# A fixed order for all engines in the second half of a down-projection

## The chip, the cores and the metric

The kernel runs on one core of a Trainium2 chip. The metric is the device time of one execution in microseconds, lower is better. All data are float32; one launch computes the whole layer.

## The reference, cut to what matters

The layer is a hybrid of two recurrent mixers with a convolutional feed-forward block behind them. The change lies in the last piece: the down-projection of the feed-forward block, its residual sum and the final norm.

```python
def _conv_ffn(h, w_up, conv_w, w_down, rows, cols):
    u = _dwconv2d(h @ w_up, conv_w, rows, cols)
    a, b = jnp.split(u, 2, axis=-1)
    return (jax.nn.silu(a) * b) @ w_down          # (1024, 2816) @ (2816, 1024)

xl = xl + g2 * _conv_ffn(...)                     # residual sum, (1024 tokens, 1024)
return _rmsnorm(xl, final_norm_w)                 # y * rsqrt(mean(y*y) + EPS) * w
```

## The kernel before

The engines are called V (VectorE), S (ScalarE), G (GpSimd), PE (TensorE) and SY (SyncE, which issues the DMAs). `P` is 128, `D` is 1024, `NLT` is 8 (blocks of 128 tokens), `NF` is 22 (slices of 128 rows of the inner width 2816), `NL` is 4.

Float32 products are made in three matmuls of a short float format (`F32R`): an operand is split into a high part, which is a cast (`S.copy`), and a low part, which is the operand less its high part. `gh` and `gl` are the parts of the activations `Gt[c]` (128 x 1024), `wh` and `wl` those of the weights (128 x 512). The three products are (gh, wh), (gh, wl), (gl, wh).

`down_ops(c, dh, kind)` (L1500 to L1524) makes the four parts for slice c and output half dh: a DMA brings the weights of two slices into `wst` (three buffers), S casts `wh` (L1520) and `gh` (L1522), G subtracts for `wl` (L1521), V for `gl` (L1523). With kind 1, `gh` and `gl` go into two pairs of buffers (tags L0 to L3) that alternate with c, so that the parts of slice c can be written when the matmuls of slice c-2 have ended. With kind 2 the parts go into buffers of their own, in the places of activations that are no longer read, so that four slices are kept at once.

The output has 1024 columns and is made in two halves (`dh` 0 and 1) of 512. In each half all eight token blocks are summed up in PSUM at once, which fills it. In the loop over slices (L1578 to L1584) each slice gives 24 matmuls (three for each of eight blocks). In the first half this loop runs over all 22 slices. In the second half it runs over 18, and for the last four (`rest`, L1585) the order is turned: block by block, the 12 matmuls of four slices, so that each block can be finished while the next is computed.

Behind the first half come, for each block: `evac` (V multiplies the PSUM result by the gate `g2bc` into `ytmp`, L1595), `acc` (V adds it to the residual `ys`, L1600; S squares the sum and adds it up into `s0`, L1602), and a multiplication of the sum by the norm weight `fnw` on G (L1611). Behind each block of the second half comes `evac` and `acc` again and then `final`: G adds the two sums of squares, scales and adds EPS, and takes the power -1/2 (L1615 to L1617), S and V scale the two halves (L1618, L1619), SY issues the output DMA (L1620). `final` of block t-1 is written behind `acc` of block t.

A list scheduler decides the order of the instructions of each engine, save within `tc.manual_schedule(engines=...)`: there the engines named keep the order of the program text. Before, this held for PE in the whole down-projection, and for PE and V from L1623, the blocks of the last four slices, on. S, G and SY were ordered by the scheduler.

Of the kernel before, what the change touches and what calls it, by code (L numbers as in the profile page):

```python
# [9 lines left out]
F32 = mybir.dt.float32  # L10
F32R = mybir.dt.float32r
I32 = mybir.dt.int32
AF = mybir.ActivationFunctionType
ALU = mybir.AluOpType
# [3 lines left out]
P = 128  # L18
D = 1024
# [5 lines left out]
NLT = T // P  # L25
# [6 lines left out]
EPS = 1e-6  # L32
# [43 lines left out]
def kernel(ctx: ExitStack, tc: tile.TileContext, A: dict, out: bass.AP):  # L76
    nc = tc.nc
    ms_cm = tc.manual_schedule(engines={mybir.EngineType.PE})
    ms_cm.__enter__()
    V, S, G, PE, SY = nc.vector, nc.scalar, nc.gpsimd, nc.tensor, nc.sync  # L80

    def pool(name, bufs=1, space=None, side=None):
        kw = {}
        if space is not None:
            kw["space"] = space
        if side is not None:
            kw["side"] = side
        return tc.tile_pool(name=name, bufs=bufs, **kw)
# [3 lines left out]
    def take(units, n):  # L92
        for _ in range(n):
            next(units, None)
# [21 lines left out]
    neghalf = cst[:, P + 89:P + 96]  # L116
# [82 lines left out]
    for k in range(KD):  # L199
        for g, gs in enumerate(x7g):  # L200
            if k == 0:
                S.activation(ssq[g], xk[k][:, gs], AF.Square)
            elif k == KD - 1 or g == 0:
                w_ = gs if k == KD - 1 else slice(0, T)
                n_ = w_.stop - w_.start
                sq = sp2.tile([P, T], F32, name="sq", tag="ld", bufs=8)
# [193 lines left out]
    order = [*range(KD // 2, KD), *range(KD // 2)]  # L400
    for k in range(KD):
        n = k + 2
# [232 lines left out]
    with ExitStack() as es:  # L635
# [12 lines left out]
        acc = [0.0, 0.0]  # L648
# [191 lines left out]
        def ml_prep(h, qt):  # L840
            Wt = []
            Qs = []
            for d in range(2):
                g4 = ml4.tile([P, NLT, P], F32, name="g4", tag="w4")
                SY.dma_start(out=g4, in_=gdv[h, d * 16 + NCX:d * 16 + NCH, :].partition_broadcast(P))
                w4 = ml4.tile([P, NLT, P], F32, name="w4t", tag="w4")
                V.tensor_tensor(w4, g4, mmask[:, d, :].unsqueeze(1).to_broadcast([P, NLT, P]), op=ALU.max)
                for c in range(NLT):
                    S.activation(w4[:, c, :], w4[:, c, :], AF.Exp, scale=-1.0, bias=U[:, d, NCX + c, h:h + 1])
                G.tensor_tensor(g4, g4, M[:, d, NCX:NCH, h:h + 1].to_broadcast([P, NLT, P]), op=ALU.subtract)  # L850
                S.activation(g4, g4, AF.Exp, scale=-1.0)
                V.tensor_tensor(g4, g4, qt.rearrange("p (c t) -> p c t", c=NLT), op=ALU.mult)
                Wt.append(w4)
                Qs.append(g4)
            return Wt, Qs
# [110 lines left out]
        pre = ml_prep(0, cur["q"])  # L966
        run(rnd1)
        flips = None
        for h in range(H):
# [12 lines left out]
            pre = None  # L982
# [360 lines left out]
    with ExitStack() as es:  # L1343
# [56 lines left out]
        ms_cm = tc.manual_schedule(engines={mybir.EngineType.PE, mybir.EngineType.Activation})  # L1400
# [52 lines left out]
    def big_tile(i, name):  # L1453
        return pl_tile(name) if i % 4 < 2 else psb.tile([P, T], F32, name=name, tag="plb")
# [7 lines left out]
    with ExitStack() as es:  # L1462
# [36 lines left out]
        def down_ops(c, dh, kind):  # L1499
            if c % 2 == 0:  # L1500
                st = wp.tile([P, 2, 512], F32, name="wst", bufs=3)
                SY.dma_start(out=st, in_=A["wdown"][dh, c // 2].rearrange("p (a b) -> p a b", a=2))
                pst["s"] = st
                if kind == 2:
                    pst["w"] = [g_pool(c - NF + NL + i).tile([P, 2, 512], F32R, name="wd", tag=f"G{c - NF + NL + i}")
                                for i in range(2)]
            src = pst["s"][:, c % 2, :]
            if kind == 2:
                wh, wl = [w[:, c % 2, :] for w in pst["w"]]
                gh, gl = [g_pool(j).tile([P, T], F32R, name="gd", tag=f"G{j}")  # L1510
                          for j in range(NL + 2 * (c - NF + NL), NL + 2 * (c - NF + NL) + 2)]
            else:
                wh = wp.tile([P, 512], F32R, name="wh", bufs=4)
                wl = wp.tile([P, 512], F32R, name="wl", bufs=4)
                if kind:
                    gh, gl = [lo.tile([P, T], F32R, name="gd", tag=f"L{2 * (c % 2) + i}") for i in range(2)]
                else:
                    gh = Gr.tile([P, T], F32R, name="gh")
                    gl = Gr.tile([P, T], F32R, name="gl")
            S.copy(wh, src)  # L1520
            G.tensor_tensor(wl, src, raw(wh), op=ALU.subtract)  # L1521
            S.copy(gh, Gt[c])  # L1522
            (G if dh == 0 and c < 3 else V).tensor_tensor(gl, Gt[c], raw(gh), op=ALU.subtract)  # L1523
            return gh, gl, wh, wl  # L1524
# [30 lines left out]
    dn_ = ctx.enter_context(pool("dn", bufs=2, side="right"))  # L1555
    d1 = ctx.enter_context(pool("d1", bufs=1, side="right"))
    fnw = d1.tile([P, D], F32, name="fnw")
    SY.dma_start(out=fnw, in_=A["fnw"].partition_broadcast(P))
    ms_cm = tc.manual_schedule(engines={mybir.EngineType.PE})
    ms_cm.__enter__()  # L1560
    ys = [lo.tile([P, D], F32, name=f"y{t}", tag=f"L{4 + t}") for t in range(NLT)]
    s0 = d1.tile([P, NLT, 2], F32, name="s0")
    pre = [pre0]
    for dh in range(2):
        ds_ = slice(dh * 512, (dh + 1) * 512)
        pp = [big_tile(i, "pd") for i in range(NLT // 2)]
        po = [pp[t % 4][:, (t // 4) * 512:(t // 4 + 1) * 512] for t in range(NLT)]

        def part(c, last, dh=dh):
            return down_ops(c, dh, 2 if last else 1)  # L1570

        def mm(t, c, gh, gl, wh, wl):
            ts_ = slice(t * P, (t + 1) * P)
            for pi, (x, w) in enumerate(((gh, wh), (gh, wl), (gl, wh))):
                PE.matmul(po[t], x[:, ts_], w,  # L1575
                          start=(c == 0 and pi == 0), stop=(c == NF - 1 and pi == 2))

        n = NF - NL * dh  # L1578
        for c in range(n):
            if dh == 0 and 6 <= c < 6 + NLT:  # L1580
                SY.dma_start(out=ys[c - 6], in_=x1d[c - 6])
            ops = pre.pop(0) if pre else part(c, False)
            for t in (0, 4, 1, 5, 2, 6, 3, 7):
                mm(t, c, *ops)  # L1584
        rest = [part(c, True) for c in range(n, NF)]  # L1585

        yt = []
        slots = itertools.cycle(range(12, 16))

        def evac(t):  # L1590
            if not yt:
                pair = lo.tile([P, T], F32, name="ytmp", tag=f"L{next(slots)}")
                yt.extend((pair[:, 0:512], pair[:, 512:1024]))
            tmp = yt.pop(0)
            V.tensor_tensor(tmp, po[t], g2bc[:, ds_], op=ALU.mult)  # L1595
            return tmp

        def acc(t, tmp):
            y = ys[t][:, ds_]
            V.tensor_tensor(y, y, tmp, op=ALU.add)  # L1600
            sq = dn_.tile([P, 512], F32, name="fsq")
            S.activation(sq, y, AF.Square, accum_out=s0[:, t, dh:dh + 1])  # L1602
            return y

        if dh == 0:
            order = (0, 4, 1, 5, 2, 6, 3, 7)
            tmps = [evac(t) for t in order]
            pre = [part(c, False, 1) for c in range(2)]
            for t, tmp in zip(order, tmps):
                y = acc(t, tmp)  # L1610
                G.tensor_tensor(y, y, fnw[:, ds_], op=ALU.mult)  # L1611
            continue
        def final(t, y):
            rs = dn_.tile([P, 2], F32, name="rs")
            G.tensor_tensor(rs[:, 0:1], s0[:, t, 0:1], s0[:, t, 1:2], op=ALU.add)  # L1615
            G.tensor_scalar(rs[:, 0:1], rs[:, 0:1], 1.0 / D, EPS, op0=ALU.mult, op1=ALU.add)
            G.tensor_tensor(rs[:, 1:2], rs[:, 0:1], neghalf[:, 0:1], op=ALU.pow)  # L1617
            S.activation(ys[t][:, 0:512], ys[t][:, 0:512], AF.Copy, scale=rs[:, 1:2])  # L1618
            V.scalar_tensor_tensor(y, y, rs[:, 1:2], fnw[:, ds_], op0=ALU.mult, op1=ALU.mult)  # L1619
            SY.dma_start(out=out[t * P:(t + 1) * P, :], in_=ys[t])  # L1620

        ms_cm.__exit__(None, None, None)
        ms_cm = tc.manual_schedule(engines={mybir.EngineType.PE, mybir.EngineType.DVE})  # L1623
        ms_cm.__enter__()
        pend = None
        for t in range(NLT):
            for i, ops in enumerate(rest):
                mm(t, n + i, *ops)
            cur = (t, acc(t, evac(t)))
            if pend is not None:  # L1630
                final(*pend)
            pend = cur
        final(*pend)
    ms_cm.__exit__(None, None, None)


# [81 lines left out]
```

## Time and profile before

| | us |
|---|---|
| median of 3 runs | 1572.02 |
| lowest and highest run | 1570.85, 1574.15 |
| profiled execution, its time | 1571.65 |
| its span, first to last instruction | 1569.8 |
| TensorE busy in the span | 1498.0 |
| first down-projection matmul | 1305.7 |

The time of an execution is taken on the device and is a little longer than the span, which goes from the first to the last instruction in the profile. PE stands for matmuls, PEld for their weight loads, DVE for VectorE, ACT for ScalarE, POOL for GpSimd, SP for SyncE. All positions are microseconds from the start of the span. PEclk is the clock granted to TensorE as a share of 2.4 GHz; 0.50 is 1.2 GHz.

### The profile page before, as it was taken

What the parts mean: (1) busy time and instruction counts of PE and PEld (TensorE: products, weight loads), DVE (VectorE), ACT (ScalarE), POOL (GpSimd) and SP (SyncE); (2) the same over time, 40 slices, a digit from 0 to 9 for tenths busy, and PEclk for the clock granted to TensorE, in tenths of its full rate; (3) what the DMA queues carried; (4) which work ended last, traced back from release to release, by engine and by line L of the source; (5) the groups of instructions that cost most, each with busy time, mean ns of one, the idle gap of its engine ahead of it and who ended that gap; (6) DMA issues with size and microseconds to landing.
All of it is one profiled execution on the core that took longest, in us unless ns stands there. A gap on an engine that the chain in (4) does not pass through costs nothing.

```text
span 1569.8 us, 22515 instructions
## 1 busy us (share of the span) xinstructions
PE 1498.0 (95%) x8934; PEld 1216.9 (78%) x8934; DVE 1112.2 (71%) x1460; ACT 543.4 (35%) x949; POOL 599.6 (38%) x510
## 2 busy tenths in 40 slices
PE   7899999998999999999999999999999998998997
PEld 4667788887877777777867888888888886886886
DVE  5777667779486776766587988989889898226334
ACT  4443243444143243434454222222222223233332
POOL 0073244554244644433322433332333325335341
PEclk8999999999999999999999999999999999999999
DMA  9246430222031111125567111111111104111102
GB/s 377 84 145 199 145 98 28 80 68 55 33 119 55 56 42 44 39 82 173 176 213 287 41 54 41 54 50 45 54 41 54 52 30 160 58 50 41 51 30 108
DMA packets 47935, 141.78 MB, mean 90 GB/s; under 512 B 4947, under 2 KB 15059, under 8 KB 47830
## 3 DMA queue, kind: packets, MB, share of 16 engines
q1 hardware_dynamic: 47830, 140.35, 26.5%
q8 instruction: 70, 1.15, 0.3%
q14 instruction: 35, 0.29, 0.1%
HBM read 119.81 MB, written 12.13 MB: 84 GB/s over the span
## 4 chain that ended last, share of the span: by engine, by line
PE 70%; DVE 7%; POOL 3%; ACT 3%; issue 2%; DMA 1%; POOLq 0%; SPq 0%; ACTq 0%; DVEq 0%
PE pu L1429 30%; PE pd L1575 13%; PE po L1285 3%; PE pl_hg L509 3%; PE pl_zb L509 3%; PE pl_zf L509 3%; PE pl_mo L509 2%; PE pl_mq L509 2%; PE pc L509 1%; PE pl_hq L509 1%; PE ap L1088 1%; DVE G L1490 1%; POOL QQ L1125 1%; PE st L876 1%; PE pl_mk L509 1%
## 5 line engine op out<-in xcount | busy, mean ns | idle before, releaser
L1429 PE MATMUL pu<-low,wh 128*128 128x512 f32 x1216 | 374.2, 389 | 0.0
L133 ACT CAST wh<-wst 128x512 fp32r<-128x512 f32 x184 | 112.0, 620 | 527.9 <-issue 227.2
L135 POOL TENSOR_TENSOR wl<-wst,wh 128x512 fp32r<-128x512 f32 x114 | 150.8, 1325 | 356.0 <-ACT wh L133 343.0
L1429 PEld LDWEIGHTS pu<-low,wh 128*128 128x128 f32 x1216 | 228.2, 188 | 47.4
L1429 PE MATMUL pu<-low,wl 128*128 128x512 f32 x608 | 236.5, 389 | 0.0
L1490 DVE SCALAR_TENSOR_TENSOR G<-pu,fcw,G 128x945 f32<-128x945 f32 (+2 forms) x168 | 205.3, 1222 | 23.9 <-ACT G L1483 19.1
L1490 DVE SCALAR_TENSOR_TENSOR cb<-pu,fcw,cb 128x945 f32<-128x945 f32 (+2 forms) x168 | 205.3, 1222 | 23.6 <-ACT cb L1483 18.8
L1575 PE MATMUL pd<-wh,gd 128*128 128x512 f32 x624 | 195.8, 395 | 11.6 <-DVE gd L1523 6.7
L1523 DVE TENSOR_TENSOR gd<-G,gd 128x1024 fp32r<-128x1024 f32 x41 | 56.8, 1386 | 129.7 <-ACT gd L1522 129.5
L1575 PEld LDWEIGHTS pd<-wh,gd 128*128 128x128 f32 x624 | 118.8, 191 | 37.9 <-DVE gd L1523 7.8
L1125 POOL TENSOR_TENSOR QQ<-QQ,FF 128x256 f32<-128x256 f32 x112 | 108.8, 993 | 80.7 <-PE ap L1088 38.0
L1429 PEld LDWEIGHTS pu<-low,wl 128*128 128x128 f32 x608 | 114.1, 188 | 23.7
L1575 PE MATMUL pd<-wl,gd 128*128 128x512 f32 x312 | 122.8, 394 | 0.0
L1521 POOL TENSOR_TENSOR wl<-wst,wh 128x512 fp32r<-128x512 f32 x40 | 73.2, 1833 | 113.8 <-ACT wh L1520 113.8
L135 DVE TENSOR_TENSOR wl<-wst,wh 128x512 fp32r<-128x512 f32 x70 | 57.7, 844 | 58.1 <-ACT wh L133 57.9
L1522 ACT CAST gd<-G 128x1024 fp32r<-128x1024 f32 x43 | 45.0, 1049 | 131.4 <-PE pd L1575 124.8
L1575 PEld LDWEIGHTS pd<-wl,gd 128*128 128x128 f32 x312 | 59.6, 191 | 12.5
L1118 DVE TENSOR_TENSOR KK<-KK,FF 128x768 f32<-128x768 f32 (+1 forms) x56 | 52.2, 942 | 15.2 <-PE tps L1104 11.8
L1552 POOL TENSOR_TENSOR G<-G,cb 128x1024 f32<-128x1024 f32 x22 | 53.9, 2452 | 14.9 <-DVE cb L1490 14.9
L874 POOL TENSOR_SCALAR kw<-ktok,WS 128x128 f32<-128x128 f32 x60 | 25.2, 422 | 49.2 <-PE st L876 48.9
L330 POOL TENSOR_TENSOR wl<-wst,wh 128x512 fp32r<-128x512 f32 x18 | 31.6, 1775 | 30.8 <-ACT wh L328 22.0
L1081 ACT COPY X<-KK 128x512 f32<-128x512 f32 x40 | 26.9, 682 | 47.0 <-DVE KK L1118 34.0
(390 smaller groups left out, 3078.3 us busy)
## 6 DMA issues: line engine op xcount, KB each, us to landing
wst<-in_wup_dram SPq DMA_DIRECT2D x44, 512.0 KB, 3.3
wst<-in_wcm_dram SPq DMA_DIRECT2D x28, 512.0 KB, 3.4
wst<-in_wmod_dram SPq DMA_DIRECT2D x26, 512.0 KB, 3.4
wst<-in_wout_dram SPq DMA_DIRECT2D x24, 512.0 KB, 3.6
wst<-in_wdown_dram SPq DMA_DIRECT2D x22, 512.0 KB, 3.4
wst<-in_wvml_dram SPq DMA_DIRECT2D x10, 512.0 KB, 6.0
x<-in_xcT_dram SPq DMA_DIRECT2D x8, 512.0 KB, 6.3
wsh<-in_wsh_dram SPq DMA_DIRECT2D x8, 512.0 KB, 10.1
```

The lines of the kernel that those rows point to most:

```text
L133: S.copy(wh, st[:, hs_])
L135: (eng or G).tensor_tensor(wl, st[:, hs_], raw(wh), op=ALU.subtract)
L509: PE.matmul(o, w[:, ws], x[k][:, c0:c1], start=(k == 0 and pi == 0), stop=(k == KD - 1 and pi == 2))
L1118: V.tensor_tensor(kv, kv, tk, op=ALU.mult)
L1125: G.tensor_tensor(qv, qv, tq, op=ALU.mult)
L1285: PE.matmul(po[g], x[k][:, ts_], halves[g][wi], start=(k == 0 and pi == 0), stop=(k == KD - 1 and pi == 2))
L1429: PE.matmul(pl[:, gs], w[:, ws], x[k][:, gs], start=(k == 0 and pi == 0), stop=(k == KD - 1 and pi == 2))
L1490: V.scalar_tensor_tensor(a3[:, r0:r1, c0:c1], s3[:, r0 + dy:r1 + dy, c0 + dx:c1 + dx], wcol((dy + 1) * 3 + dx + 1), a3[:, r0:r1, c0:c1], o ...
L1521: G.tensor_tensor(wl, src, raw(wh), op=ALU.subtract)
L1523: (G if dh == 0 and c < 3 else V).tensor_tensor(gl, Gt[c], raw(gh), op=ALU.subtract)
L1552: G.tensor_tensor(Gt[j], Gt[j], cb, op=ALU.mult)
L1575: PE.matmul(po[t], x[:, ts_], w, start=(c == 0 and pi == 0), stop=(c == NF - 1 and pi == 2))
```

## The change

From the end of the first half on, PE, V, S and G all keep the order of the text. The parts of slice 0 of the second half are written before the eight evacuations of the first, the parts of slice 1 behind them, and in the loop the parts of slice c+2 behind the matmuls of slice c. The eight `acc` of the first half, which stood behind the evacuations, become a generator (`sums`), of which two are taken in each of the slices 0 to 3. The eight multiplications by `fnw` become another (`scaled`), one for each slice from 4 on, each with a small G instruction that adds EPS to the first half's sum of squares. The division by D goes into the square (`scale=D ** -0.5`). `final` loses one G instruction, and the last block's output goes out in two DMAs of 512 columns, one issued by S and one by SY. The parts of slices 18 to 21 (`rest`) stand behind the loop, as before, but are now held to that order.

```diff
-    s0 = d1.tile([P, NLT, 2], F32, name="s0")
+    s0 = d1.tile([P, NLT, 4], F32, name="s0")
...
             for t in (0, 4, 1, 5, 2, 6, 3, 7):
                 mm(t, c, *ops)
+            if dh and c + 2 < n:
+                pre.append(part(c + 2, False))
+                take(late[0], 2)
+                if c > 3:
+                    take(late[1], 1)
         rest = [part(c, True) for c in range(n, NF)]
...
-            S.activation(sq, y, AF.Square, accum_out=s0[:, t, dh:dh + 1])
+            S.activation(sq, y, AF.Square, scale=D ** -0.5, accum_out=s0[:, t, dh:dh + 1])
             return y
 
         if dh == 0:
             order = (0, 4, 1, 5, 2, 6, 3, 7)
+            ms_cm.__exit__(None, None, None)
+            ms_cm = tc.manual_schedule(engines={mybir.EngineType.PE, mybir.EngineType.DVE, mybir.EngineType.Activation,
+                                                mybir.EngineType.Pool})
+            ms_cm.__enter__()
+            pre = [part(0, False, 1)]
             tmps = [evac(t) for t in order]
-            pre = [part(c, False, 1) for c in range(2)]
-            for t, tmp in zip(order, tmps):
-                y = acc(t, tmp)
-                G.tensor_tensor(y, y, fnw[:, ds_], op=ALU.mult)
+            pre.append(part(1, False, 1))
+
+            def sums(todo, acc=acc):
+                for t, tmp in todo:
+                    acc(t, tmp)
+                    yield
+
+            def scaled(fs=fnw[:, ds_]):
+                for t in order:
+                    y = ys[t][:, 0:512]
+                    G.tensor_scalar(s0[:, t, 0:1], s0[:, t, 0:1], 1.0, EPS, op0=ALU.mult, op1=ALU.add)
+                    G.tensor_tensor(y, y, fs, op=ALU.mult)
+                    yield
+
+            late = (sums(list(zip(order, tmps))), scaled())
             continue
-        def final(t, y):
-            rs = dn_.tile([P, 2], F32, name="rs")
-            G.tensor_tensor(rs[:, 0:1], s0[:, t, 0:1], s0[:, t, 1:2], op=ALU.add)
-            G.tensor_scalar(rs[:, 0:1], rs[:, 0:1], 1.0 / D, EPS, op0=ALU.mult, op1=ALU.add)
-            G.tensor_tensor(rs[:, 1:2], rs[:, 0:1], neghalf[:, 0:1], op=ALU.pow)
-            S.activation(ys[t][:, 0:512], ys[t][:, 0:512], AF.Copy, scale=rs[:, 1:2])
-            V.scalar_tensor_tensor(y, y, rs[:, 1:2], fnw[:, ds_], op0=ALU.mult, op1=ALU.mult)
-            SY.dma_start(out=out[t * P:(t + 1) * P, :], in_=ys[t])
-
-        ms_cm.__exit__(None, None, None)
-        ms_cm = tc.manual_schedule(engines={mybir.EngineType.PE, mybir.EngineType.DVE})
-        ms_cm.__enter__()
+
+        def final(t, y, one=True):
+            G.tensor_tensor(s0[:, t, 3:4], s0[:, t, 0:1], s0[:, t, 1:2], op=ALU.add)
+            rs = dn_.tile([P, 1], F32, name="rs")
+            G.tensor_tensor(rs, s0[:, t, 3:4], neghalf[:, 0:1], op=ALU.pow)
+            S.activation(ys[t][:, 0:512], ys[t][:, 0:512], AF.Copy, scale=rs)
+            if not one:
+                S.dma_start(out=out[t * P:(t + 1) * P, 0:512], in_=ys[t][:, 0:512])
+            V.scalar_tensor_tensor(y, y, rs, fnw[:, ds_], op0=ALU.mult, op1=ALU.mult)
+            if one:
+                SY.dma_start(out=out[t * P:(t + 1) * P, :], in_=ys[t])
+            else:
+                SY.dma_start(out=out[t * P:(t + 1) * P, 512:1024], in_=y)
...
             pend = cur
-        final(*pend)
+        final(*pend, False)
```

## Rows read from the trace of the kernel before

**Rows 1.** The page, parts 1 and 2: busy time by engine, and the busy share of matmuls and the granted clock in 40 slices of the span, in tenths.
```profile
PE 1498.0 (95%) x8934; PEld 1216.9 (78%) x8934; DVE 1112.2 (71%) x1460; ACT 543.4 (35%) x949; POOL 599.6 (38%) x510
...
PEclk8999999999999999999999999999999999999999
```

**Rows 2.** Busy time by engine in stages of the second half: start and end, length, busy time and (x) instructions of each engine, then granted clock, DMA share and GB/s. The stages are: chunks 0 and 1; the stop; chunk 2; chunks 3 to 17; the last four slices by blocks; the rest of the span.
```profile
1433.59:1444.49 10.90, 10.90 (x49) 8.82 (x47) 10.90 (x11) 5.01 (x13) 7.87 (x5) 1.00 0.15 51
1444.49:1449.54 5.05, 0.16 (x1) 0.00 (x0) 3.27 (x3) 3.14 (x8) 5.05 (x4) 0.89 0.00 0
1449.54:1458.14 8.60, 8.13 (x24) 6.07 (x25) 3.85 (x2) 1.94 (x3) 6.23 (x4) 0.67 0.16 49
1458.14:1539.74 81.60, 81.60 (x362) 67.59 (x361) 27.16 (x18) 27.23 (x34) 27.52 (x16) 1.00 0.11 34
1539.74:1561.90 22.16, 22.16 (x98) 17.87 (x96) 13.67 (x20) 9.41 (x20) 5.69 (x19) 1.00 0.29 119
1561.90:1569.80 7.90, 0.05 (x1) 0.00 (x0) 2.80 (x4) 2.06 (x4) 1.81 (x6) 0.66 0.49 199
```

**Rows 3.** The list of waits from 1340 to 1570: who waited for whom, total us, times, longest us.
```profile
ACT gd L1522 <- PE pd L1575: 109.7, 30, 6.7
...
PEld pd L1575 <- ACT gd L1522: 5.3, 1, 5.3
```

**Rows 4.** The timeline of ScalarE around the boundary of the halves: start, duration, line, operation, count, and in brackets the idle time before and who ended it. The casts of L1522 write `gh` of chunk 0, 1, 2, 3 and 4 of the second half, in this order.
```profile
1428.14 1.05 ACT L1522 CAST gd<-G 128x1024 fp32r<-128x1024 f32 x1 [3.87 <-PE pd L1575]
1433.59 1.05 ACT L1522 CAST gd<-G 128x1024 fp32r<-128x1024 f32 x1 [3.87 <-PE pd L1575]
1438.10 0.63 ACT L1602 ACTIVATE fsq<-y 128x512 f32<-128x512 f32 x1 [2.94 <-DVE y L1600]
...
1447.83 0.63 ACT L1602 ACTIVATE fsq<-y 128x512 f32<-128x512 f32 x1 [0.95 <-DVE y L1600]
1448.46 1.03 ACT L1522 CAST gd<-G 128x1024 fp32r<-128x1024 f32 x1
1449.40 0.61 ACT L1520 CAST wh<-wst 128x512 fp32r<-128x512 f32 x1
1449.92 1.04 ACT L1522 CAST gd<-G 128x1024 fp32r<-128x1024 f32 x1
...
1458.19 1.05 ACT L1522 CAST gd<-G 128x1024 fp32r<-128x1024 f32 x1 [6.71 <-PE pd L1575]
```

**Rows 5.** The timelines of VectorE and GpSimd around the same place, a run of like instructions merged into one row.
```profile
1429.23 1.23 DVE L1523 TENSOR_TENSOR gd<-G,gd 128x1024 fp32r<-128x1024 f32 x1 [4.17 <-ACT gd L1522]
1430.37 4.87 DVE L1595 TENSOR_TENSOR ytmp<-pd,g2bc 128x512 f32<-128x512 f32 x8
...
1436.29 11.45 DVE L1600 TENSOR_TENSOR y<-y,ytmp 128x512 f32<-128x512 f32 x8
...
1438.90 11.19 POOL L1611 TENSOR_TENSOR y<-y,fnw 128x512 f32<-128x512 f32 x7 [1.38 <-ACT fsq L1602]
...
1452.27 3.50 POOL L1521 TENSOR_TENSOR wl<-wst,wh 128x512 fp32r<-128x512 f32 x2
```

**Rows 6.** The chain of work that ended last, from 1427 to 1455, in order of time: start, us, what.
```profile
1436.29 2.99 DVE y L1600 x4
...
1440.90 6.85 DVE y L1600 x4
```

**Rows 7.** All instructions of two lines: count, duration in ns (min/median/max), first and last start.
```profile
L1523 DVE TENSOR_TENSOR gd<-G,gd x41: 1215/1226/2296, 1327.7 to 1530.0; 128x1024 fp32r<-128x1024 f32 x41
...
L1521 POOL TENSOR_TENSOR wl<-wst,wh x40: 1277/1809/2286, 1271.0 to 1519.7; 128x512 fp32r<-128x512 f32 x40
```

**Rows 8.** The timeline of the end, behind the last matmul (blocks 6 and 7).
```profile
1562.72 0.69 DVE L1600 TENSOR_TENSOR y<-y,ytmp 128x512 f32<-128x512 f32 x1
1562.98 0.72 ACT L1618 ACTIVATE y<-y,rs 128x512 f32<-128x512 f32 x1 [1.22 <-POOL rs L1617]
...
1563.60 0.61 ACT L1602 ACTIVATE fsq<-y 128x512 f32<-128x512 f32 x1
...
1564.39 0.19 POOL L1615 TENSOR_TENSOR rs<-s 128x1 f32<-128x1 f32 x1 [1.45 <-ACT fsq L1602]
1564.67 0.19 POOL L1616 TENSOR_SCALAR rs<-rs 128x1 f32<-128x1 f32 x1
1564.94 0.55 POOL L1617 TENSOR_TENSOR rs<-rs,cst 128x1 f32<-128x1 f32 x1
1565.53 0.72 ACT L1618 ACTIVATE y<-y,rs 128x512 f32<-128x512 f32 x1 [1.22 <-POOL rs L1617]
1565.53 0.75 DVE L1619 SCALAR_TENSOR_TENSOR y<-y,rs,fnw 128x512 f32<-128x512 f32 x1 [1.46 <-POOL rs L1617]
```

**Rows 9.** The output DMAs of blocks 6 and 7: their issue on SP, and the DMA share (second figure from the end) and GB/s (last) in stages behind the issue of block 7.
```profile
1564.15 0.33 SPq L1620 DMA_DIRECT2D out_dram<-y  x1
...
1566.35 0.33 SPq L1620 DMA_DIRECT2D out_dram<-y  x1
...
1566.35:1567.05 0.70, 0.00 (x0) 0.00 (x0) 0.00 (x0) 0.00 (x0) 0.00 (x0) 0.50 0.00 0
1567.05:1568.45 1.40, 0.00 (x0) 0.00 (x0) 0.00 (x0) 0.00 (x0) 0.00 (x0) 0.50 0.91 375
1568.45:1569.80 1.35, 0.00 (x0) 0.00 (x0) 0.00 (x0) 0.00 (x0) 0.00 (x0) 0.50 0.00 0
```

**Rows 10.** The timeline of ScalarE, at the first of the casts for the last four slices (`wd`).
```profile
1502.88 0.62 ACT L1520 CAST wd<-wst 128x512 fp32r<-128x512 f32 x1 [5.05 <-DMA wst<-in_wdown_dram]
```

More of the change, by code (lines that the diff above doesn't have):

```diff
@@ L1596, in evac, with acc @@
             return tmp
-        def acc(t, tmp):
+        def acc(t, tmp, dh=dh, ds_=ds_):
             y = ys[t][:, ds_]
```

## The prediction

> **What bounds the kernel now.** I read the page first, for who is busy: TensorE has 95% of the span and a clock near full [rows 1]. Moving work between the other engines is then worth only what it takes off TensorE's idle time, off time at its low clock, or off the piece after its last matmul. So I cut the region of the change into stages [rows 2]. The second half of the down-projection is 22 chunks (a chunk: one 128-row slice of the weights, 24 matmuls over all eight token blocks). In the long undisturbed stage 15 chunks take 81.60 us, 5.44 each, at granted clock 1.00. Its chunks 0 and 1 take 10.90, the same pace. Then comes a stage of 5.05 us in which TensorE does almost nothing, and chunk 2 takes 8.60 us at a mean clock of 0.67, so partly at 1.2 instead of 2.4 GHz. The loss is 5.05 + (8.60 - 5.44) = 8.21 us. Check: from 1433.59, where the second half begins, 18 chunks would end at 1433.59 + 18 x 5.44 = 1531.51; they end at 1539.74, 8.23 later. After that nothing is lost until the last matmul at 1561.9, and 7.9 us follow it.
>
> Next, who is late at that stop. The list of waits names it: TensorE's weight load waited once, 5.3 us, for the ScalarE cast that makes the high part of the activations, `gh` of L1522 [rows 3]. The long waits of that cast for TensorE (30 of them, 109.7 us) are another thing: the `gh` buffer is double, so the cast for chunk c+2 starts when chunk c has ended, a full chunk ahead of need. The one for chunk 2 could have started when chunk 0 ended, 1433.59 + 5.44 = 1439.03. It started at 1448.46 [rows 4], since the eight sums of squares of the first half stand in front of it in ScalarE's queue, the first at 1438.10 and the last at 1447.83, with gaps between. Those gaps come from VectorE, which makes the eight sums `y + tmp` from 1436.29 on in 11.45 us [rows 5]. The chain shows why so long: the first four take 2.99 us, 0.75 each, the last four 6.85, 1.71 each [rows 6]; from 1438.90 on GpSimd multiplies the same rows by the norm weight, 11.19 us for seven [rows 5]. So a block of side work, due only at the end, holds the split that TensorE needs.
>
> **The change, part by part.**
>
> *Order at the boundary.* The split of chunk 0 comes first, then the eight evacuations, then the split of chunk 1. VectorE does just this now: the low part at 1429.23, evacuations from 1430.37 [rows 5], and TensorE passes from one half to the other without a stop [rows 2]. Nothing gained or lost. The cast of the weights (`wh`) now stands before `gh` instead of behind; it has no late input, so it and `wl` come earlier.
>
> *Splits two ahead, sums spread.* After chunk c's matmuls come the split of c+2 and then two sums, for c = 0 to 3; the multiplications by the norm weight follow one per chunk from c = 4 to 11. Now what a pass costs, as the queues are in order. From the start of `gh`: 1.09 until the low part starts (1428.14 to 1429.23), 1.14 until VectorE is free for the next (1429.23 to 1430.37), two sums at 0.75, one square of 0.63 behind the second, 0.52 from `wh` to the next `gh` (1449.40 to 1449.92) [rows 4 to 6]. Together 4.88, under the 5.44 of a chunk, so the next `gh` waits for TensorE and not for the sums. The split itself is whole 1.09 + 1.23 = 2.32 after chunk c ends [rows 4, 7] and needed 5.44 later (its low part 0.45 later still, as third matmul): a margin of 3.1 to 3.6. GpSimd has one `wl` (1.81) and then one multiplication (11.19 / 7 = 1.60) per chunk, with a very small instruction for EPS: some 3.6 of 5.44. So the stop goes whole: minus 8.2. What is late next is nothing on TensorE, if a pass stays under 5.44. In the passes with sums, `wl` is released by `wh`, which stands behind the squares; it runs beside casts and low parts, not beside the sums, so I take 0.75 for a sum. The far bound is 1.71.
>
> The port is the point to weigh. The rows show 0.75 against 1.71 for one and the same sum without and with GpSimd's multiplication beside it [rows 6]. The Trainium skill ("SBUF — State Buffer", section "Who interferes with whom") says that a VectorE instruction with two SBUF inputs and a GpSimd instruction that reads SBUF exclude each other for a whole instruction. By that rule the low part could wait for all of a `wl` in each pass, and the forecast would be that of rival B.
>
> *The last four splits.* Chunks 18 to 21 use other buffers. Now their casts slip into free time; in the fixed order they stand behind the split of chunk 17, whose `gh` waits for chunk 15. Counted from that end: `gh` 17 lasts 0.96, four pairs of casts take 4 x (0.52 + 0.96) = 5.9, the last low part ends 1.2 to 2.3 later [rows 4, 7], so 8.1 to 9.2. The first block's matmuls with row 18 begin 10.88 after it, with row 21 2.0 later. GpSimd's four `wl` at 1.81 to 2.29 are 7.2 to 9.2, starting 1.6 in, ready at 8.8 to 10.8 [rows 7]. Hidden; cover left, 2 us or more.
>
> *The end.* For each block one GpSimd instruction goes: 0.27, from 1564.67 to 1564.94 [rows 8]. The order on ScalarE is now: square of block t, then scaling of block t-1. At block 7 the square starts right behind its sum, which ends at 1562.72 + 0.69 = 1563.41, so at 1563.45 instead of 1563.60: minus 0.15. The last scaling starts 0.42 earlier, at 1565.11 on the old time axis. But the scaling of block 6 moves from 1562.98 to behind that square: 1563.45 + 0.63 = 1564.08, ending 1564.80, and its output DMA is issued at 1564.87 instead of 1564.15. An output moves its 512 KB in 1.40 us, from 0.70 after its issue [rows 9]. Block 6 then moves from 1565.57 to 1566.97, and block 7, issued at 1565.11 + 0.75 + 0.07 = 1565.93, until 1568.37 if they follow each other, or 1568.03 if they didn't disturb each other. Before: 1568.45. So minus 0.1 to 0.4. I take 0.1, since the 375 GB/s of that stage is about what the DMA engines move whenever they are full. Splitting the last output over two issuing engines gives nothing by itself: both halves are ready within 0.03 (0.72 and 0.75). Its rows become 2 KB; no row shows a store of that form. If a packet costs the same at half its size, 1.40 is lost; below, the gain is 0.4. The nearest row, the 1.40 for the same bytes, speaks for no change.
>
> *Sum.* 8.2 + 0.1 = 8.3, against the profiled execution: 1571.65 - 8.3 = 1563.35 (span 1569.8, and the 1.85 around it stays). The median of the runs shown is 1572.02, 0.37 above it, which would give 1563.7. I forecast 1563.5.
>
> **Rivals.**
>
> A, the forecast, 0.78: 1563.5, own range 1562 to 1565.
>
> B, the sums are slowed after all, 0.08. At 1.71 a pass takes 4.88 + 1.92 = 6.8, 1.36 too long; after four passes the split is 5.4 late, less the margin of 3.6: TensorE stops for 1.9 in chunks 5 and 6. Time 1565.4, and up to 1568.5 where the clock falls once (3.16). For: the row of 1.71. Against: it belongs to the multiplications, which now come later. The skill's rule gives the same place: one `wl` of 1.81 in each pass, 6.7.
>
> C, slower, 0.05: the same mechanism at its worst. With 1.71 per sum and 2.30 for the low part [rows 7] a pass takes about 8.0, 2.5 too long. After four passes that is 10, less 2.5 of margin: 7.5 of stops, spread over chunks 4 to 6, and if the clock falls at each, 3 x 3.16 more: 17 lost, about 1580. It decides from a pass of some 7 us on: below that the loss stays under the 8.3 gained. Against: GpSimd has only one `wl` per pass there.
>
> D, the last four splits come late, 0.05. The first cast of their weights waited 5.05 us for its DMA [rows 10]. If that came after chunk 15's end, 8.1 to 9.2 become 13.2 to 14.2, where 13.3 are to be had (10.88 + 2.0 + 0.45): a stop of up to 1, and the clock 3.16. Time 1564 to 1567.5. Against: in the new order that cast comes at 1433.59 + 16 x 5.44 + 1.0 = 1521.6 of the old time axis and not at 1502.88, and its load can start as soon as its buffer is free, long before.
>
> E, the change doesn't do what it says, 0.04: chunk 2 was late for something else as well, for instance its `wl`, made from 1452.27 on by GpSimd behind the multiplications [rows 5], and a new wait takes the place. Time 1571.5. Against: the one long wait is put down to the cast, and the order moves `wl` too.
>
> **How the numbers follow.** Within 0.2% is 3.1 us, about what a measurement of this kernel can tell. Faster by more: A, nearly all of B and D: 0.89. Within: E and the upper edges: 0.06. Slower: C, 0.05. The range goes from 1561.8 (the end gains its 0.4, with the 1.2 by which the lowest run shown lies under the median) to 1567.0 (B and most of D, or the end's bad bound of 1.4): some 0.85 by the cases, less what I can't see.
>
> **What would show it.** In the changed profile: no wait of TensorE over 1 us between the halves, granted clock 1.00 from the first chunk of the second half to the last; `gh` of chunk 2 starting within 0.1 us of the end of chunk 0; two sums at about 0.75 behind each of the low parts of chunks 2 to 5; the last output issued about 0.4 earlier behind the last matmul, but the data ending only 0.1 earlier. I am wrong if VectorE's sums stay at 1.5 or more, if a wait of TensorE for a low part or for the weights of chunks 18 to 21 appears, or if the clock falls somewhere in the half without a stop.

## The result, and the profile after

| | before | after |
|---|---|---|
| median | 1574.04 us (6 runs) | 1564.22 us (6 runs) |
| lowest to highest | 1570.85 to 1577.89 | 1560.47 to 1568.68 |
| ratio | | 0.9931, 95% interval 0.9907 to 0.9955 |
| profiled execution, span | 1569.8 | 1558.7 |
| from the end of the first half to the end of the span | 136.21 | 127.79 |

The kernel became faster by 0.7%, with an interval of 0.45% to 0.93%, 7.1 to 14.6 us. A second series of the same code (11 runs before, 6 after) gave 0.9943 (0.9928 to 0.9958). The forecast was 1563.5, or 8.3 us less.

The stages of the second half are cut as in [rows 2]: chunks 0 and 1; chunk 2; chunks 3 to 17; the last four slices by blocks; the rest.

```profile
1430.91:1441.79 10.88, 10.88 (x49) 9.01 (x48) 5.21 (x7) 4.47 (x8) 2.86 (x2) 1.00 0.08 30
1441.79:1447.23 5.44, 5.44 (x25) 4.50 (x24) 2.43 (x3) 2.90 (x7) 1.18 (x2) 1.00 0.31 96
1447.23:1528.83 81.60, 81.60 (x361) 67.57 (x360) 27.90 (x22) 30.01 (x43) 44.19 (x34) 1.00 0.12 39
1528.83:1550.95 22.12, 22.12 (x97) 17.82 (x95) 14.03 (x21) 8.58 (x20) 4.76 (x14) 1.00 0.29 119
1550.95:1558.70 7.75, 0.04 (x1) 0.00 (x0) 2.80 (x4) 2.24 (x5) 1.21 (x3) 0.80 0.51 203
```

There is no stage for a stop any more: TensorE is busy in every microsecond from the end of the first half to the last matmul, at granted clock 1.00. Chunk 2 takes 5.44 us like every other, where the stop and chunk 2 took 5.05 + 8.60. The other stages are the same within 0.04, and the end is 0.15 shorter. Together 8.42 us. The spans of these rows have one decimal; with two, the piece from the start of the last evacuation on went from 7.85 to 7.65, by 0.2.

The span fell by 11.1 us, 2.7 more than these stages explain. That part lies ahead of the change, in code whose order is the same on every engine: the first matmul of the down-projection starts at 1302.4 here and at 1305.7 before. It moves from execution to execution (see the last section), and the profiled execution of after happened to be the fastest of the six.

The timelines of ScalarE and VectorE around the boundary answer to [rows 4, 5]. The casts of L1522 here are those of chunks 2 and 3.

```profile
1436.35 1.05 ACT L1522 CAST gd<-G 128x1024 fp32r<-128x1024 f32 x1 [3.87 <-PE pd L1575]
1439.30 0.63 ACT L1607 ACTIVATE fsq<-y 128x512 f32<-128x512 f32 x1 [1.89 <-DVE y L1605]
...
1440.54 0.60 ACT L1520 CAST wh<-wst 128x512 fp32r<-128x512 f32 x1
1441.84 1.05 ACT L1522 CAST gd<-G 128x1024 fp32r<-128x1024 f32 x1 [0.70 <-PE pd L1575]
...
1437.43 1.23 DVE L1523 TENSOR_TENSOR gd<-G,gd 128x1024 fp32r<-128x1024 f32 x1 [3.74 <-ACT gd L1522]
1438.58 1.29 DVE L1605 TENSOR_TENSOR y<-y,ytmp 128x512 f32<-128x512 f32 x2
```

The cast for chunk 2 starts at 1436.35, when chunk 0 has ended (1430.91 + 5.44), where it started 9.4 us late before. A sum now takes 0.65 us (1.29 for two), less than the 0.75 of the estimate. From the start of `gh` to the next `wh` a pass takes 1440.54 - 1436.35 = 4.19, with the 0.52 of that cast 4.7; the next `gh` waits the last 0.70 us for TensorE, as it should.

At the end, the last block's timeline, a stretch in which the DMA engines are busy (share and GB/s are the last two figures), and the whole piece from the start of the last evacuation:

```profile
1552.54 0.63 ACT L1607 ACTIVATE fsq<-y 128x512 f32<-128x512 f32 x1 [1.41 <-DVE y L1605]
...
1553.16 0.71 ACT L1639 ACTIVATE y<-y,rs 128x512 f32<-128x512 f32 x1
...
1554.19 0.72 ACT L1639 ACTIVATE y<-y,rs 128x512 f32<-128x512 f32 x1 [0.32 <-POOL rs L1638]
...
1554.60:1557.30 2.70, 0.00 (x0) 0.00 (x0) 0.35 (x1) 0.32 (x1) 0.00 (x0) 0.70 0.97 386
...
1551.03:1558.68 7.65, 0.00 (x0) 0.00 (x0) 2.80 (x4) 2.16 (x5) 1.13 (x3) 0.80 0.51 206
```

Block 6's scaling (1553.16) stands behind block 7's square, and from 1554.60 to 1557.30 the DMA engines are full: two outputs, one behind the other, at 386 GB/s. The last output is ready 0.4 earlier than before, and its data end only some 0.2 earlier. The two issues of the last output start at 1554.94 and 1554.98, 0.40 long on ScalarE and 0.33 on SP.

### The profile page after: what moved, and what is told of

Same layout as the page of the kernel before. It is cut to its first block, busy times and chain, and to the rows that moved or that the text cites. A ratio compares the mean times of both kernels' runs of the same rounds, so it can differ in the third digit from the quotient of the medians.

```text
span 1558.7 us, 22522 instructions
## 1 busy us (share of the span) xinstructions
PE 1492.2 (96%) x8934; PEld 1212.8 (78%) x8934; DVE 1102.0 (71%) x1460; ACT 542.4 (35%) x949; POOL 596.4 (38%) x510
## 4 chain that ended last, share of the span: by engine, by line
PE 71%; DVE 6%; POOL 3%; issue 3%; ACT 2%; DMA 2%; POOLq 0%; ACTq 0%; DVEq 0%; SPq 0%
PE pu L1429 30%; PE pd L1575 13%; PE po L1285 3%; PE pl_hg L509 3%; PE pl_zb L509 3%; PE pl_zf L509 3%; PE pl_mo L509 2%; PE pl_mq L509 2%; PE pc L509 1%; PE pl_hq L509 1%; PE ap L1088 1%; DVE G L1490 1%; PE pl_mk L509 1%; POOL QQ L1125 1%; DMA g<-gd 1%
## 5 line engine op out<-in xcount | busy, mean ns | idle before, releaser
L1522 ACT CAST gd<-G 128x1024 fp32r<-128x1024 f32 x43 | 45.0, 1050 | 138.2 <-PE pd L1575 134.6
```

## The experiments

All lengths below are taken in the profile from the start of the `gh` cast for chunk 1 of the second half (the end of the first half) to the end of the span. Three profiles of kernels with the changed order gave 127.79, 127.74 and 127.86, so 0.3 us can be told there, while whole times move by several us.

**Was it the place of the sums and multiplications?** They go back ahead of the split of chunk 2.

```diff
             if dh and c + 2 < n:
+                if c == 0:
+                    for _ in range(NLT):
+                        take(late[0], 1)
+                        take(late[1], 1)
                 pre.append(part(c + 2, False))
-                take(late[0], 2)
-                if c > 3:
-                    take(late[1], 1)
```

> The changed kernel, with the eight sums and the eight multiplications by the norm weight put back ahead of the split of chunk 2, each sum with its multiplication, in the fixed order; all else is kept. Measured is the length from the end of the first half (start of the cast gh for chunk 1) to the end of the span: 136.2 us in the kernel before, 127.8 in the changed one. Theory (the sums and multiplications in front of the split make the stop): 136 us, give or take 0.7, with a TensorE stop of about 5 us ahead of chunk 2 and some 3 us at the lower clock behind it. Rival (the fixed order of ScalarE and GpSimd or the new end made the gain): 128 to 129.

Measured: 1576.7 - 1435.82 = 140.9 us. So the gain goes, and 4.7 us more. The waits of TensorE for `wl` from 1436 on, the stages around the stop, VectorE's eight sums and the cast for chunk 2:

```profile
PEld pd L1575 <- POOL wl L1521: 9.7, 1, 9.7
PE pd L1575 <- POOL wl L1521: 9.4, 1, 9.4
...
1446.70:1448.50 1.80, 0.69 (x2) 0.19 (x1) 0.55 (x1) 1.80 (x4) 1.56 (x3) 1.00 0.00 0
1448.50:1458.00 9.50, 0.11 (x1) 0.11 (x1) 2.14 (x2) 1.40 (x2) 8.92 (x10) 0.68 0.00 0
...
1438.53 7.11 DVE L1606 TENSOR_TENSOR y<-y,ytmp 128x512 f32<-128x512 f32 x8
...
1446.88 1.04 ACT L1522 CAST gd<-G 128x1024 fp32r<-128x1024 f32 x1
```

TensorE stops 1.1 us for the `gh` cast and then 9.4 us for `wl` of chunk 2, which in the fixed order stands behind all eight multiplications on GpSimd. The scheduler had put that one ahead of them. So holding all engines to the text was no gain by itself; with the old place in the text it costs. The theory had the sign and missed the size, since it followed only one of the three queues. Nor does the run repeat the stop of before: the sums took 7.11 us here and not 11.45, and the cast for chunk 2 was 5.6 us late (1435.82 + 5.44 = 1441.26) and not 9.4. It shows that the block costs time in that place, and not by which queue it did so before; that is read from the trace of before [rows 3, 4].

**Is the place enough, without the multiplications beside the sums?**

```diff
             if dh and c + 2 < n:
+                if c == 0:
+                    take(late[0], NLT)
                 pre.append(part(c + 2, False))
-                take(late[0], 2)
```

> The changed kernel with the eight sums ahead of the split of chunk 2, but the multiplications left where the change put them, in chunks 4 to 11. Theory of the port (the stop needs the multiplications beside the sums, which make each sum 1.7 us instead of 0.65): eight sums take 5.2 us, the last square ends some 5.8 us after the low part of chunk 1, the split of chunk 2 is ready within 0.5 us of need; 127.8 to 128.5 us from the end of the first half, no stop. Rival (the place in the queue is enough): a stop of 2 to 5 us and a fall of the clock, 132 to 136.

Measured: 1566.6 - 1438.50 = 128.1 us, no stop over 0.4 us. VectorE's sums and the casts of chunk 2 and 3:

```profile
1441.21 4.90 DVE L1606 TENSOR_TENSOR y<-y,ytmp 128x512 f32<-128x512 f32 x8
...
1447.39 1.05 ACT L1522 CAST gd<-G 128x1024 fp32r<-128x1024 f32 x1
1449.38 1.05 ACT L1522 CAST gd<-G 128x1024 fp32r<-128x1024 f32 x1 [0.42 <-PE pd L1575]
...
PEld pd L1575 <- DVE gd L1523: 0.4, 1, 0.4
```

The eight sums take 4.90 us, 0.61 each, where they took 11.45 beside the multiplications [rows 5]. The cast for chunk 2 is still some 3.4 us late and that is nearly all the margin there is: only the low part makes TensorE wait, 0.4 us. So the place alone didn't make the stop. It needed the multiplications, which more than doubled the time of the sums.

**Is the spreading needed?** All eight sums stand behind the split of chunk 2.

```diff
                 pre.append(part(c + 2, False))
-                take(late[0], 2)
+                if c == 0:
+                    take(late[0], NLT)
```

> The changed kernel with all eight sums behind the split of chunk 2 instead of two behind each of four splits. Theory (ahead or behind the next split is what counts, not the spreading): the cast of chunk 3 is late by some 3 us, its low part ready about when it is needed; 127.8 to 128.5 us from the end of the first half. Rival (the spreading is needed): a stop of 1 us or more ahead of chunk 3, 129 to 133.

Measured: 1561.8 - 1434.04 = 127.8 us, and no wait of TensorE in the second half. The casts for chunks 3 and 4:

```profile
1447.91 1.05 ACT L1522 CAST gd<-G 128x1024 fp32r<-128x1024 f32 x1
...
1450.36 1.05 ACT L1522 CAST gd<-G 128x1024 fp32r<-128x1024 f32 x1 [0.89 <-PE pd L1575]
```

The cast for chunk 3 comes at 1447.91, 3.0 late, and the next at 1450.36 is in time again. Two sums in each of four passes are no better than eight in one, as long as the multiplications come later.

**Is the fixed order of ScalarE and GpSimd needed?** Only TensorE and VectorE are held to the text.

```diff
-            ms_cm = tc.manual_schedule(engines={mybir.EngineType.PE, mybir.EngineType.DVE, mybir.EngineType.Activation,
-                                                mybir.EngineType.Pool})
+            ms_cm = tc.manual_schedule(engines={mybir.EngineType.PE, mybir.EngineType.DVE})
```

> The changed kernel with the text as it is, but only TensorE and VectorE held to it; ScalarE and GpSimd are ordered by the scheduler as before. Theory (the place in the text does it, by way of VectorE's order): no stop, 127.6 to 128.3 us from the end of the first half. Rival (the fixed order on all engines is needed): squares or multiplications come ahead of a cast again, a stop of 1 us or more.

Measured: 1562.5 - 1434.92 = 127.6 us. No wait of TensorE in the second half either, though the scheduler put the multiplications (L1628) back beside the sums and the low parts. VectorE's rows, then two of GpSimd:

```profile
1448.08 3.48 DVE L1605 TENSOR_TENSOR y<-y,ytmp 128x512 f32<-128x512 f32 x2
1453.35 2.36 DVE L1523 TENSOR_TENSOR gd<-G,gd 128x1024 fp32r<-128x1024 f32 x1 [1.79 <-ACT gd L1522]
1455.63 2.39 DVE L1605 TENSOR_TENSOR y<-y,ytmp 128x512 f32<-128x512 f32 x2
...
1442.01 1.81 POOL L1521 TENSOR_TENSOR wl<-wst,wh 128x512 fp32r<-128x512 f32 x1 [3.15 <-ACT wh L1520]
...
1445.48 1.31 POOL L1628 TENSOR_TENSOR y<-y,fnw 128x512 f32<-128x512 f32 x1
```

Two sums take 2.4 to 3.5 us instead of 1.29, and a low part up to 2.36 instead of 1.23; the margin holds it. The `wl` of 1442.01 is already that of chunk 4, whose matmuls begin at 1434.92 + 4 x 5.44 = 1456.68: with ScalarE and GpSimd free, `wl` stays far ahead. So the place in the text does it, and the fixed order of ScalarE and GpSimd adds nothing to it here.

**Rival B and C, made to happen.** The multiplications come right behind the sums, two and two in each of the chunks 0 to 3, all engines fixed.

```diff
                 pre.append(part(c + 2, False))
-                take(late[0], 2)
-                if c > 3:
-                    take(late[1], 1)
+                for _ in range(2):
+                    take(late[0], 1)
+                    take(late[1], 1)
```

> The changed kernel with the multiplications taken in the same passes as the sums, each right behind its sum (two and two in each of chunks 0 to 3), as the rival of the slowed sums supposes. Theory (a pass has room): the second sum of a pass and the next low part lie beside a multiplication and take up to 1.7 and 2.3 us, a pass stays under or near 5.44 us; no stop over 0.5 us, 127.8 to 128.5 us from the end of the first half. Rival (the port decides also when spread): passes of 6.8 us and more, stops of 2 us or more in chunks 4 to 6, 130 to 140.

Measured: 1561.9 - 1431.44 = 130.5 us, 2.7 more than without. VectorE's timeline, TensorE's waits, the `wl` of chunk 5, and the stages in which the waits lie:

```profile
1449.59 2.27 DVE L1523 TENSOR_TENSOR gd<-G,gd 128x1024 fp32r<-128x1024 f32 x1 [2.33 <-ACT gd L1522]
1451.78 2.38 DVE L1605 TENSOR_TENSOR y<-y,ytmp 128x512 f32<-128x512 f32 x2
1456.48 2.28 DVE L1523 TENSOR_TENSOR gd<-G,gd 128x1024 fp32r<-128x1024 f32 x1 [2.33 <-ACT gd L1522]
...
PE pd L1575 <- POOL wl L1521: 2.1, 2, 1.2
...
1457.65 2.25 POOL L1521 TENSOR_TENSOR wl<-wst,wh 128x512 fp32r<-128x512 f32 x1
...
1459.00:1462.00 3.00, 2.10 (x10) 1.71 (x10) 2.05 (x2) 1.46 (x5) 1.47 (x3) 1.00 0.35 105
...
1465.00:1470.00 5.00, 3.84 (x18) 2.84 (x17) 2.12 (x2) 1.57 (x2) 5.00 (x3) 1.00 0.01 3
```

A pass now takes 6.89 us (1449.59 to 1456.48): the low part 2.27, a sum 1.19. The rival had 6.8, from other terms. TensorE stops twice, 2.1 us in all, for `wl`, in line with its 1.9, in the chunks 5 and 6 that it named; the other 0.6 us of the 2.7 are not traced to anything. The theory's "no stop" was wrong. The slowing of rival B is real, and the change avoids it by taking the multiplications later. But it made a stop only where ScalarE and GpSimd keep the order of the text: the `wl` of chunk 5 stands behind two multiplications and ends at 1459.90, when that chunk has begun at 1431.44 + 5 x 5.44 = 1458.64, while in the run before this one, with sums as slow and the two engines free, TensorE never waited. The granted clock stayed at 1.00 through both stops, so the 3 x 3.16 us that made rival C slower than before did not come with them.

**The end of the kernel before, in the fixed order.** Three GpSimd instructions per block and one last output.

```diff
+            G.tensor_scalar(rs[:, 0:1], rs[:, 0:1], 1.0, 0.0, op0=ALU.mult, op1=ALU.add)
...
-        final(*pend, False)
+        final(*pend)
```

> The changed kernel with the end of the kernel before: three GpSimd instructions for each block instead of two (the scaling multiplies by 1 and adds 0, since EPS is in already), and the last output in one DMA. Measured is the piece behind the last evacuation's start (1561.99 to the end of the span before, 7.81 us; 7.67 in the changed kernel). Theory (the output data of blocks 6 and 7 follow each other on the DMA engines): the last output is issued 0.27 later, its data still start as block 6's end, 7.6 to 7.8. Rival (the chain of small instructions sets the end): 7.9 to 8.0.

Measured: 7.77 us from the start of the last evacuation, against 7.65 in the changed kernel (7.67 above, with a span of one decimal). The last scaling starts at 1554.41 and not 1554.13 on this axis (1554.19 less 0.06), 0.28 later, yet the data still fill one stretch:

```profile
1554.60:1557.30 2.70, 0.00 (x0) 0.00 (x0) 0.56 (x1) 0.53 (x1) 0.00 (x0) 0.51 0.94 387
...
1550.96:1558.73 7.77, 0.00 (x0) 0.00 (x0) 2.80 (x4) 2.16 (x5) 1.52 (x5) 0.74 0.49 203
```

So the shorter chain of instructions and the two DMAs are together worth 0.1 us of the 0.28: the DMA engines, full at 387 GB/s, take the rest. The theory's 7.6 to 7.8 held.

**Block 6's output out of the way.** ScalarE scales block t-1 ahead of the square of block t.

```diff
...
             V.tensor_tensor(y, y, tmp, op=ALU.add)
+            if t:
+                rs = final(t - 1)
             sq = dn_.tile([P, 512], F32, name="fsq")
             S.activation(sq, y, AF.Square, scale=D ** -0.5, accum_out=s0[:, t, 1:2])
...
```

> The changed kernel with ScalarE's scaling of block t-1 ahead of the square of block t. Measured is the piece behind the start of the last evacuation (7.67 in the changed kernel). Theory (block 6's output, held behind the square of block 7, keeps the DMA engines busy when block 7 is ready): block 6 is issued 0.7 earlier, block 7 as now, 7.35 to 7.45. Rival (the two don't disturb each other): 7.6 to 7.8, or more if the square is held up by the scaling.

Measured: 7.52 us. It is a gain of 0.13, half of what the theory gave, and lies between the ranges of theory and rival. The two outputs no longer run in one full stretch:

```profile
1560.50:1561.90 1.40, 0.00 (x0) 0.00 (x0) 0.70 (x1) 0.67 (x1) 0.00 (x0) 1.00 0.72 293
1561.90:1563.35 1.45, 0.00 (x0) 0.00 (x0) 0.00 (x0) 0.00 (x0) 0.00 (x0) 0.70 0.91 353
...
1557.28:1564.80 7.52, 0.00 (x0) 0.00 (x0) 2.79 (x4) 2.17 (x4) 1.14 (x3) 0.85 0.52 209
```

Where only TensorE and VectorE were held to the text, the scheduler had put block 6's scaling ahead of that square too, and the piece took 7.50. But it did not come every time: the last version below has the same end, and there the piece took 7.79. The last output by itself takes 1.45 us at 353 GB/s (1.40 at 375 for the undivided one, [rows 9]); it was not worse for its two halves by more than 0.05.

**The same sort of stop, in the first half.** The changed kernel still stops 6.2 us ahead of chunk 3 of the first half, for a low part that stands behind convolutions on VectorE.

```diff
-            (G if dh == 0 and c < 3 else V).tensor_tensor(gl, Gt[c], raw(gh), op=ALU.subtract)
+            (G if dh == 0 and c < 5 else V).tensor_tensor(gl, Gt[c], raw(gh), op=ALU.subtract)
...
-            G.tensor_tensor(Gt[j], Gt[j], cb, op=ALU.mult)
+            (V if j == NF - 1 else G).tensor_tensor(Gt[j], Gt[j], cb, op=ALU.mult)
```

> The changed kernel, and in the first half the low parts of chunks 3 and 4 on GpSimd instead of VectorE, and the last multiplication of the convolution on VectorE instead of GpSimd. There TensorE stops for 6.2 us ahead of chunk 3, for a low part that stands behind convolution work in VectorE's queue, and runs some 3 us at the lower clock after it. Theory (the same sort of stop, side work ahead of a split): the stop falls under 1 us and the clock stays, so the stretch from the first matmul of the down-projection to the end of its first half is 8 to 9 us shorter. Rival (GpSimd is late in turn, since its weights' low parts and these contend with VectorE's convolutions): 2 to 6 us shorter, with a wait for GpSimd.

Measured: the stretch went from 128.5 to 126.4 us. The ten profiles with this part unchanged gave 127.7 to 129.1, so it is 1.3 to 2.7 shorter: the size is the rival's at its lower edge, not the theory's. The wait is not the rival's: TensorE waits 4.2 us for VectorE and 0.2 for GpSimd. The stop moved to chunk 5, and the first row says why:

```profile
1313.59 17.72 DVE L1490 SCALAR_TENSOR_TENSOR cb<-src,fcw,cb 128x1008 f32<-128x1008 f32 x8 [2.29 <-ACT cb L1483]
1331.34 1.23 DVE L1552 TENSOR_TENSOR G<-G,cb 128x1024 f32<-128x1024 f32 x1
1332.48 3.42 DVE L1523 TENSOR_TENSOR gd<-G,gd 128x1024 fp32r<-128x1024 f32 x2
```

The convolutions take 2.2 us each, with GpSimd at work beside them, where they took 1.5 in the changed kernel, and a multiplication follows. So the low part of chunk 5 starts 30.4 us after the first matmul, 8.3 later than that of chunk 3 did (22.0), which uses up most of the 10.9 that two chunks give. One more low part for GpSimd (`c < 6`), together with ScalarE's scaling ahead of the square as in the experiment on block 6's output, is the version that beats both the kernel before and the changed one; it was measured beside the changed kernel.

> The changed kernel again, on one chip beside the next one. From the stages of the two profiles (8.4 us less in the second half) a ratio of 0.9947 to the kernel before, 0.993 to 0.996.

> The changed kernel with ScalarE's scaling ahead of the square, and the low parts of chunks 3, 4 and 5 of the first half on GpSimd, the last multiplication of the convolution on VectorE. In e4_first_half the stop went from chunk 3 (6.2 us) to chunk 5 (4.2), behind convolutions on VectorE that were slower (17.7 us for eight) beside GpSimd's work. Theory: GpSimd makes the low part of chunk 5 some 2 us late, VectorE that of chunk 6 in time; the clock may not fall; the first half 5 to 8 us shorter than in the changed kernel (128.5 from its first matmul to the end), a ratio of 0.990 to 0.992 to the kernel before. Rival: the stop moves on to chunk 6, 1 to 3 us shorter, a ratio of 0.9925 to 0.9945.

Measured, against the kernel before: the changed kernel 0.9943 (0.9928 to 0.9958), 1563.99 us; the new one 0.9908 (0.9891 to 0.9925), 1558.17 us. Its first half takes 1428.83 - 1307.5 = 121.3 us, against 128.5 and 129.1 in two profiles of the changed kernel, as the theory had it (5 to 8 us, a ratio of 0.990 to 0.992). Two waits are left of the stop, shorter than the 2 us it had; the third row is the piece from the last evacuation on:

```profile
PE pd L1575 <- DVE gd L1523: 0.7, 1, 0.7
PE pd L1575 <- POOL gd L1523: 0.2, 1, 0.2
...
1548.94:1556.73 7.79, 0.00 (x0) 0.00 (x0) 2.80 (x4) 2.17 (x4) 1.14 (x3) 0.68 0.51 203
```

So its gain is all in the first half. At the end, block 7's square starts 1.07 us after the start of its sum (1549.67, 1550.74), where it was 0.79 in the run with the same end (1558.00, 1558.79). What held it there is open.

## Why the prediction was right

*The time.* 1563.5 lies 0.7 from the median of 1564.22, and that is in part luck: the medians differ by 9.8 us and not by 8.3, and the median before, over six runs, is 1574.04, 2.0 above that of the three runs from which the forecast started. What can be held against the forecast of 8.3 are the lengths of the stages, 8.4.

*The stop.* The term was 8.21 to 8.23 and measured 8.27 in the stages up to the last matmul (8.42 less the end's 0.15). That side work ahead of the split of chunk 2 stops TensorE is shown by the run that puts it back, though there mostly by way of `wl`; that before it was the cast is read from the trace. What the prediction left open is settled: ahead of the split, the block made a stop of 5 us because the multiplications stretched it. Without these there is 0.4 us of waiting.

*A pass of 4.88 against a chunk of 5.44.* It was 4.7. The margin was taken from single durations, and all of them held, since the sums had no GpSimd work beside them, as argued.

*The port.* The page "SBUF — State Buffer" of the Trainium skill (section "Who interferes with whom") puts VectorE and GpSimd in each other's way, and the traces agree: 0.61 to 0.65 for a sum alone, 1.19 to 1.7 beside multiplications. The step from there to rival B took a `wl` beside the low part in every pass. In the changed kernel there was none in the passes with sums: `wl` of chunk 3 ran from 1441.22 to 1442.52, behind the sums and ahead of the low part of 1442.93, and the two took their short times, 1.30 and 1.23. In the chunks with multiplications and low parts only, nothing was late. With the multiplications in the chunks of the sums, rival B came about at the size given (stops of 2.1 for 1.9), but through `wl` on GpSimd and not through the low part on VectorE.

*The last four splits.* Nothing came late, but one length was wrong. Four low parts took 8.70 us and four `wl` 8.53, since the two engines worked beside each other:

```profile
1519.59 8.53 POOL L1521 TENSOR_TENSOR wd<-wst,wd 128x512 fp32r<-128x512 f32 x4 [3.63 <-ACT wd L1520]
...
1520.50 8.70 DVE L1523 TENSOR_TENSOR gd<-G,gd 128x1024 fp32r<-128x1024 f32 x4 [0.25 <-ACT gd L1522]
```

Counted from the end of chunk 15 (1430.91 + 16 x 5.44 = 1517.95), `wl` was ready at 10.2, within the 8.8 to 10.8 of the forecast. The last low part ended at 11.2 (1529.20), not at 8.1 to 9.2: the prediction added a single low part to the casts, but at 2.18 each the four of them follow one another more slowly than the casts, at 1.48. It was needed at 10.88 + 2.0 + 0.45 = 13.3. So 2 us of cover were left, as forecast, but on VectorE's side and not on GpSimd's, where the forecast had its least; that the number fits is luck.

*The end.* 0.15 to 0.2 for a forecast of 0.1. The chain became 0.4 shorter and the DMA engines gave back half of it or more, by the step that the prediction named: block 6's output behind block 7's square.

*Slips.* Rival E pointed at `wl` from 1452.27 on. Counted in order, those two were for chunks 4 and 5, and that of chunk 2 had been made from 1429.80 on, long in time. The cast `wh` and its `wl` were to come earlier; those of chunk 2 came later (`wl` at 1432.56, 1.65 after the end of the first half, where it was 3.79 ahead of it), and it cost nothing. And rival C's price was made with a fall of the clock at every stop, which the stops of 0.90 and 1.16 us didn't bring.

## What to carry to other kernels

Work that is due late, written in one block ahead of a split that the next stage needs, cost little here (0.4 us) until something stretched it: look for the split's own wait, and then for what makes the work in front of it slow. Taking the slow neighbour away was nearly enough. Moving the block behind the split, with the neighbour still beside it, left no stop where ScalarE and GpSimd were free to keep `wl` ahead, and stops of 2.1 us where they were held to the text; doing both left none. So follow every queue that the block stands in, since fixing the order of an engine also fixes what stands behind it. At the end of a program, an output that is issued late by a reordering can cost the time that a shorter chain has won.

## What the runs showed of the hardware that was not expected

Two stops of TensorE of 0.90 and 1.16 us left the granted clock at 1.00. In the 5 us stop before the change it stood at 1.00 and 0.99 in the first two stretches below and at 0.50 in the last:

```profile
1444.49:1446.49 2.00, 0.16 (x1) 0.00 (x0) 2.00 (x2) 1.04 (x3) 2.00 (x2) 1.00 0.00 0
1446.49:1448.49 2.00, 0.00 (x0) 0.00 (x0) 1.25 (x1) 1.05 (x5) 2.00 (x2) 0.99 0.00 0
1448.49:1449.54 1.05, 0.00 (x0) 0.00 (x0) 0.02 (x1) 1.05 (x3) 1.05 (x2) 0.50 0.00 0
```

The run with more low parts on GpSimd is a case between them: behind its stop of 4.2 us in the first half, the granted clock was 0.52 for 3.4 us. So here two short stops of 2.1 us together came with 2.7 us of lost time, and the one of 5.05 with 8.2, of which 3.16 in the chunk behind it.

The first matmul of the down-projection started between 1302.1 and 1310.4 us in the twelve profiles, in code that was the same up to there. That is as much as the change is worth, and it is why the span of a single profile fell by 11.1 where the stages fell by 8.4. Much of it is there by the first of the `ap` matmuls (L1088), at 443.4 to 449.0 in five of them. What makes it is open.
